# Differential attention with queries on partitions, one set of scores for maxima and exponentials, and both maps combined ahead of the values

## The chip, the core and the metric

The kernel runs on one core of a Trainium2 chip. The metric is the device time of one execution in microseconds (us). The engines are named as in the profile: PE is TensorE (matmuls; PEld its weight loads), DVE is VectorE, ACT is ScalarE, POOL is GpSimd, SP is SyncE, which in this kernel issues every DMA. SBUF is the on-chip memory, PSUM the accumulators: eight banks, each 512 floats wide on 128 partitions.

## The reference

Two layers of a diffusion backbone over 2048 latent tokens and 256 context tokens, width 1024. Layer 0 has a grouped-query attention (stage A) and a neighbourhood attention (B); layer 1 has a differential attention (stage C) and a sliding-window attention (D). Each layer ends with a gated output projection. The change touches stage C, the last part of the program. What is computed there, for 4 heads, 2 maps of 64 columns each, 2304 keys and values of 128 columns:

```python
def diff_attend(q, k, v, lam):
    sc = jnp.einsum('bqhmd,bkhmd->bhmqk', q, k).astype(jnp.float32) * SCALE
    p = jax.nn.softmax(sc, axis=-1)
    a = (p[:, :, 0] - lam * p[:, :, 1]).astype(v.dtype)
    return jnp.einsum('bhqk,bkhe->bqhe', a, v)
# then, for the 2048 latent queries:
yc = (rms_norm(yc, subln) * (1.0 - lam0)).reshape(b, n_tok, -1)
y = jnp.concatenate([yc, yd], axis=-1) * jax.nn.silu(z)
x = x + gate[:, None] * (y @ w_out)
return rms_norm(x, final_norm)
```

## The kernel before

Every number that goes through PE is kept as two float16 halves, a high one (H) and a low one (L, the rest), and a product is made of two or three matmuls of halves that add up in PSUM. All matmuls but transposes go through the helper `mm` (L82).

Stage C is the second half of `layer1`, from `back_pools("C", s)` on. Its work units are (head h, block of 256 queries qb, map m): 4 x 8 x 2 = 64, run by `r_phase` (L800). Each is done in two passes over the scores:

- `r_front` (L736), two units ahead: queries on partitions. Five matmuls of 512 keys with the high half of the keys alone, for each of two tiles of 128 queries (into `pM`), each followed by a maximum on DVE (L752). The maximum is put, negated, into column 64 of a tile Z and brought by a matmul with an identity into row 64 of `Q2`, so that the second pass subtracts it within its matmul.
- `r_scores` (L766): keys on partitions. For each of 18 key tiles two matmuls of 256 queries (`KH` with `Qt`, `KL` with `Q2`), four key tiles to a tile `pS` of two banks, of which there are two. ACT takes the exponential (`Pm`, L778) and casts it to the high half (`H`, L781); POOL subtracts for the low half (`L`, L783). The exponentials lie with keys on partitions, as the product with the values wants them.
- `r_values` (L786), three groups behind: for each key tile and each 128 queries three matmuls of 128 or 129 columns (H with both halves of V, L with the high half) into `pO`. Column 128 of V is one, so that the sum of the exponentials comes with the product.
- `finish` (in `layer1`): divides by the sum. For map 1 it keeps the result times -lambda (`o`, L1454); for map 0 it adds the two (`yc`, L1463), takes the sum of squares, the power -1/2 on POOL (L121), scales and stores.

Between these units a `Filler` lets the output projection run in small steps: `part` (load, gate on POOL, L1494), then `out_pair` (L860: maximum, scaling, transposes, twelve matmuls of 512 columns for each half row, `ot` L911, `xo` L912, and for the last half `final`, L921). Rates (`rateC`, `rateE`, `rateF`) say how many steps come with a group. The order of the instructions on each engine is fixed when the program is built: a scheduler orders them by its own timeline, and on the chip each engine runs its queue in that order and waits at semaphores.

## Time and profile before

| | us |
|---|---|
| median of 3 runs | 3750.49 |
| lowest and highest | 3746.72, 3753.26 |
| the profiled execution's own time | 3762.25 |
| its span, first to last instruction | 3760.40 |
| PE busy | 3565.1 (95%) |
| DVE busy | 2603.6 (69%) |
| ACT busy | 2403.2 (64%) |
| POOL busy | 2347.4 (62%) |

The profile is of one execution. Busy times are sums of instruction durations on an engine. Queries on the trace give them by stretch (windows), by line and shape (groups), or one instruction after another (the timeline). In the groups the part after the bar is busy time and the mean duration of one, then the idle time of the engine just ahead of these instructions and what ended it. A matmul's duration in the records holds its way through the array, so starts that follow each other tell its rate. Stage C fills the last 1000 us of the span.

### The profile page before, as it was taken

How to read it: one execution, taken by the hardware profiler on the slowest of the kernel's cores; microseconds unless marked ns; L12 is line 12 of the kernel's file. 1: busy time of each engine (PE TensorE's matmuls, PEld its weight loads, DVE VectorE, ACT ScalarE, POOL GpSimd, SP SyncE). 2: the span in 40 equal slices, each digit the busy share in tenths (PEclk: the TensorE clock that was granted, in tenths of full speed). 3: DMA queues.
4: the chain of work that ended last, by engine and by line, in shares of the span. 5: the costliest groups of instructions: out<-in, count | busy, mean ns of one | idle time of the engine just before them, and what ended most of it. 6: DMA issues, size and time to landing. Idle time of an engine off the chain costs nothing. (4 is left out here: it accounts for less than half of the span.)

```text
span 3760.4 us, 103033 instructions
## 1 busy us (share of the span) xinstructions
PE 3565.1 (95%) x42242; PEld 2946.7 (78%) x42242; DVE 2603.6 (69%) x6585; ACT 2403.2 (64%) x4094; POOL 2347.4 (62%) x1822
## 2 busy tenths in 40 slices
PE   7869998989999999999999999999989999999998
PEld 5648987878976777677767888999878888887775
DVE  5746779798567676666666888777565656656666
ACT  5215655556668887787864556666567777776665
POOL 3203456676358888788864454435358878877775
PEclk9989999999999999999999999999999999999999
DMA  7884634343261111111135444412351211211222
GB/s 235 214 210 103 124 88 101 80 92 101 67 213 40 44 60 38 48 49 49 33 114 135 104 101 100 105 58 78 113 168 30 78 47 56 62 37 51 101 98 103
DMA packets 455488, 350.64 MB, mean 93 GB/s; under 512 B 207782, under 2 KB 407270, under 8 KB 454502
## 3 DMA queue, kind: packets, MB, share of 16 engines
q1 hardware_dynamic: 455014, 344.06, 33.1%
q8 instruction: 330, 5.41, 0.6%
q14 instruction: 144, 1.18, 0.1%
HBM read 207.43 MB, written 106.90 MB: 84 GB/s over the span
## 5 line engine op out<-in xcount | busy, mean ns | idle before, releaser
L783 POOL TENSOR_TENSOR L<-Pm,H 128x1024 f16<-128x1024 f32 (+1 forms) x640 | 1240.1, 1958 | 293.0 <-ACT H L781 213.1
L82 PE MATMUL pmm<-wk,hT 128*128 128x256 f16 x10848 | 1365.5, 276 | 45.4 <-DVE HL L367 19.3
L82 PEld LDWEIGHTS <-hT 128*128 128x128 f16 x10848 | 1034.9, 99 | 189.6 <-issue 35.9
L752 DVE TENSOR_REDUCE mx<-pM 128x1 f32<-128x512 f32 (+1 forms) x1280 | 787.1, 634 | 514.0 <-PE pM L82 503.8
L82 PE MATMUL pO<-V,H 128*128 128x65 f16 (+3 forms) x9216 | 785.0, 207 | 3.2 <-DVE ya L1260 1.4
L82 PEld LDWEIGHTS <-H 128*128 128x128 f16 x9216 | 644.7, 98 | 100.5 <-DVE o L1454 3.6
L82 PE MATMUL pO<-V,L 128*128 128x65 f16 (+1 forms) x4608 | 710.8, 209 | 8.0 <-POOL L L783 7.4
L514 POOL TENSOR_TENSOR Pl<-Sb,Ph 128x640 f16<-128x640 f32 (+4 forms) x288 | 439.0, 1524 | 427.5 <-ACT Ph L513 248.3
L781 ACT CAST H<-Pm 128x1024 f16<-128x1024 f32 (+1 forms) x640 | 602.9, 959 | 11.8 <-PE pO L82 1.9
L82 PE MATMUL pS<-Qt,KH 128*128 128x256 f16 x2304 | 559.1, 273 | 2.6 <-DMA KH<-qk 1.4
L82 PE MATMUL pS<-Q,KL 65*128 65x256 f16 x2304 | 550.0, 274 | 0.0
L82 PEld LDWEIGHTS <-L 128*128 128x128 f16 x4608 | 442.9, 98 | 53.1 <-POOL L L783 14.9
L82 PE MATMUL pM<-KH,Qt 128*128 128x512 f16 (+1 forms) x1280 | 448.3, 359 | 16.4 <-DVE mx L752 10.3
L778 ACT ACTIVATE Pm<-pS,esc_c 128x1024 f32<-128x1024 f32 (+1 forms) x320 | 323.3, 1026 | 207.9 <-PE pS L82 181.7
L82 PEld LDWEIGHTS <-KL 65*128 65x128 f16 x3824 | 374.4, 98 | 83.3 <-issue 28.2
L778 ACT ACTIVATE Pm<-pS,esc_a 128x1024 f32<-128x1024 f32 (+1 forms) x320 | 324.6, 1027 | 156.1 <-PE pS L82 104.0
L82 PE MATMUL pX<-wo,yT 128*128 128x512 f16 x1488 | 390.2, 380 | 1.5 <-ACT yT L890 1.3
L82 PEld LDWEIGHTS <-KH 128*128 128x128 f16 x2304 | 227.3, 99 | 59.2 <-issue 7.0
L82 PEld LDWEIGHTS <-yT 128*128 128x128 f16 x1632 | 154.2, 98 | 134.4 <-ACT yT L890 6.2
L513 ACT CAST Ph<-Sb 128x640 f16<-128x640 f32 (+4 forms) x288 | 219.4, 762 | 51.1 <-PE pO L82 41.0
L82 PE MATMUL pT<-Q,K 128*128 128x128 f16 x1520 | 216.5, 220 | 18.1 <-ACT Sb L509 6.4
L82 PE MATMUL pT<-Q,KL 65*128 65x128 f16 x1520 | 214.5, 220 | 4.4 <-DVE Q L490 4.4
(295 smaller groups left out, 5536.5 us busy)
## 6 DMA issues: line engine op xcount, KB each, us to landing
qk<-qkst SPq DMA_DIRECT2D x104, 256.0 KB, 2.4
wmod<-w_mod SPq DMA_DIRECT2D x24, 1024.0 KB, 8.4
xo<-x SPq DMA_DIRECT2D x48, 512.0 KB, 3.5
xt<-x SPq DMA_DIRECT2D x34, 512.0 KB, 4.9
G<-zz SPq DMA_DIRECT2D x68, 256.0 KB, 2.5
x<-xo SPq DMA_DIRECT2D x34, 512.0 KB, 2.9
wst<-w_in_even SPq DMA_DIRECT2D x13, 1024.0 KB, 5.8
wst<-w_in_odd SPq DMA_DIRECT2D x13, 1024.0 KB, 5.5
```

The source lines that it names most:

```text
L82: return self.nc.tensor.matmul(out=out, lhsT=l, rhs=r, start=s, stop=e, skip_group_check=skip)
L513: nc.scalar.copy(out=H[:, :n * P], in_=Sb[:, :n * P])
L514: nc.gpsimd.tensor_tensor(out=L[:, :n * P], in0=Sb[:, :n * P], in1=H[:, :n * P], op=ALU.subtract)
L752: nc.vector.tensor_reduce(out=mx[:, j:j + 1], in_=ps[:, :n], op=ALU.max, axis=AX.X)
L778: nc.scalar.activation(out=Pm[:, :n], in_=S[:, :n], func=AF.Exp, scale=esc[0], bias=LNP)
L781: nc.scalar.copy(out=H[:, :n], in_=Pm[:, :n])
L783: eng.tensor_tensor(out=L[:, :n], in0=Pm[:, :n], in1=H[:, :n], op=ALU.subtract)
```

## The change

Stage C gets its own code, with queries on partitions throughout. Its units are (head, tile of 128 queries), 64 of them, each with both maps:

- `c_map`: all 2304 scores of one map for 128 queries, two matmuls per 512 keys (keys' high and low halves, each held twice on 128 partitions, against one query tile that holds both halves), into five banks: `pSa` (1024 columns) and `pSb` (1280). There is one of each. Then three maxima from PSUM, their maximum, the shift, and two exponentials with accumulated sums, into E (32 bit, in SBUF).
- E1 times rho plus E0, with rho = -lambda times the ratio of the sums: columns 0 to 1535 on DVE in two pieces, the rest on POOL in two instructions.
- `c_halves`: of the combined rows, twelve key tiles are cast to H (ACT) and L (POOL) and brought to keys on partitions by four DMA transposes of 128x768; the other six are transposed by PE (`pTr`, one bank), and cast from there by ACT and DVE.
- `c_values`: 18 x 3 matmuls of 128 columns for both maps together, one unit later.
- `finish` scales without a division (the norm takes out the sum); the squares' small term is made on POOL. The filler runs at 5.3 or 5.4 steps a unit. The order of units changes for heads 2 and 3: block by block, so that blocks of all four heads come free early.
- The weights of the output projection come in half rows, the tile `yT` is half as wide, `px` takes turns between `pTr` and `pX` at the end.

Ahead of stage C the program keeps its instructions, but for two small scalars; in layer 1's front some of them change places. The diff, cut to its core:

```diff
-    rateC = 0.55
-    rateE = 2.0
-    rateF = 3.6
+    rateC = (5.3, 5.4)
...
+    DMAK = 12
+
+    def c_pools(self, s):
+        self.pSa = self.pool(s, "pSaC", 1, PSUM)
+        self.pSb = self.pool(s, "pSbC", 1, PSUM)
+        self.pTr = self.pool(s, "pTrC", 1, PSUM)
+        self.pX = self.pool(s, "pXC", 1, PSUM)
+        self.pO = self.pool(s, "pOC", 1, PSUM)
...
+    def c_map(self, u, m, Q, K, esc, shift):
+
+        nc = self.nc
+        S = [self.pSa.tile([P, 1024], F32, name="pSa"), self.pSb.tile([P, 1536], F32, name="pSb")]
+        mx = self.small(f"mx{m}", 3)
+        KH, KL = K
+        for i, (c0, w) in enumerate(((0, 1024), (1024, 1280))):
+            for c in range(0, w, 512):
+                n = min(512, w - c)
+                self.mm(S[i][:, c:c + n], Q, KH[:, c0 + c:c0 + c + n], True, False)
+                self.mm(S[i][:, c:c + n], Q, KL[:, c0 + c:c0 + c + n], False, True)
+        for i, (j, c, w) in enumerate(((0, 0, 1024), (1, 0, 512), (1, 512, 768))):
+            nc.vector.tensor_reduce(out=mx[:, i:i + 1], in_=S[j][:, c:c + w], op=ALU.max, axis=AX.X)
...
+        E = self.wp.tile([P, NTOK], F32, name=f"E{m}", bufs=1 + m)
+        ss = self.small(f"cs{m}", 2)
+        for i, (c0, w) in enumerate(((0, 1024), (1024, 1280))):
+            nc.scalar.activation(out=E[:, c0:c0 + w], in_=S[i][:, :w], func=AF.Exp, scale=esc[0], bias=nb,
+                                 accum_out=ss[:, i:i + 1])
+        return E, ss
+
+    def c_halves(self, E1, E0, rho):
...
+        nc.gpsimd.tensor_scalar(out=E1[:, nd:], in0=E1[:, nd:], scalar1=rho, scalar2=None, op0=ALU.mult)
+        nc.gpsimd.tensor_tensor(out=E1[:, nd:], in0=E1[:, nd:], in1=E0[:, nd:], op=ALU.add)
+        for c0, c1 in ((0, nd // 2), (nd // 2, nd)):
+            nc.vector.scalar_tensor_tensor(out=E1[:, c0:c1], in0=E1[:, c0:c1], scalar=rho, in1=E0[:, c0:c1],
+                                           op0=ALU.mult, op1=ALU.add)
+        for c0, c1 in ((0, nd // 2), (nd // 2, nd)):
+            H = self.wp.tile([P, nd // 2], F16, name="H")
+            L = self.wp.tile([P, nd // 2], F16, name="L")
+            nc.scalar.copy(out=H, in_=E1[:, c0:c1])
+            nc.gpsimd.tensor_tensor(out=L, in0=E1[:, c0:c1], in1=H, op=ALU.subtract)
+            for src, dst in ((H, HT), (L, LT)):
+                nc.sync.dma_start_transpose(out=dst[:, c0 // P:c1 // P], in_=src)
+        for k0 in range(self.DMAK, NT, 4):
+            n = min(4, NT - k0)
+            ps = self.pTr.tile([P, 512], F32, name="pTr")
+            for j in range(n):
+                nc.tensor.transpose(out=ps[:, j * P:(j + 1) * P], in_=E1[:, (k0 + j) * P:(k0 + j + 1) * P], identity=self.idf)
+            pv = ps[:, :n * P].rearrange("p (k x) -> p k x", x=P)
+            nc.scalar.copy(out=HT[:, k0:k0 + n], in_=pv)
+            nc.vector.tensor_tensor(out=LT[:, k0:k0 + n], in0=pv, in1=HT[:, k0:k0 + n], op=ALU.subtract)
+        return HT, LT
+
+    def c_values(self, O, HT, LT, V, kts):
+        for kt in kts:
+            self.mm(O, HT[:, kt], V[:, kt, P:2 * P], kt == 0, False)
+            self.mm(O, HT[:, kt], V[:, kt, 0:P], False, False)
+            self.mm(O, LT[:, kt], V[:, kt, P:2 * P], False, kt == NT - 1)
...
-            self.r_phase([(h, qb, m) for h in range(4) for qb in range(8) for m in (1, 0)], front, back, finish, 128,
-                         ((filler, lambda n: self.rateC if n < 48 else self.rateE if n < 62 else self.rateF),))
...
+            units = [(h, qt) for h in range(2) for qt in range(16)]
+            units += [(h, 2 * qb + t) for qb in range(8) for h in (2, 3) for t in range(2)]
...
+            for n, u in enumerate(units):
...
+                    E1, s1 = self.c_map(u, 1, Qs[1, h, qt // 2][:, q], ks[1], escs[h // 2], shift[1])
+                if pend:
+                    O = self.pO.tile([P, 512], F32, name="pO")[:, 0:P]
+                    self.c_values(O, *pend[1], pend[2], range(0, 9))
+                fill(n, 0.5)
+                r1 = self.small("cr1")
+                nc.vector.tensor_scalar(out=r1, in0=s1[:, 0:1], scalar1=s1[:, 1:2], scalar2=None, op0=ALU.add)
+                nc.vector.reciprocal(out=r1, in_=r1)
+                nc.gpsimd.tensor_scalar(out=r1, in0=r1, scalar1=nlam, scalar2=None, op0=ALU.mult)
+                E0, s0 = self.c_map(u, 0, Qs[0, h, qt // 2][:, q], ks[0], escs[h // 2], shift[0])
+                rho = self.small("rho")
+                nc.vector.tensor_scalar(out=rho, in0=s0[:, 0:1], scalar1=s0[:, 1:2], scalar2=r1, op0=ALU.add, op1=ALU.mult)
+                if pend:
+                    self.c_values(O, *pend[1], pend[2], range(9, NT))
+                    finish(pend[0], O, pend[3])
...
+                halves = self.c_halves(E1, E0, rho)
+                fill(n, 0.5)
+                pend = (u, halves, Vs[h], s0)
```

How the queues stand around this, first on DVE in the middle of stage C before (mx is the maximum of 512 or 256 scores in `pM`, m and Z the maximum of all and its negative, Q the row that goes into `Q2`):

```order
L752 TENSOR_REDUCE mx<-pM 128x1 x5
L755 TENSOR_REDUCE m<-mx 128x1
L758 TENSOR_SCALAR Z_50092<-m 128x1
L752 TENSOR_REDUCE mx<-pM 128x1
L764 CAST Q_59496<-pM 1x256
L752 TENSOR_REDUCE mx<-pM 128x1 x4
```

and on DVE after the change, one unit without filler from the end of its map 1 on (cr and rho are made of the sums; cm and cnb are the maximum of all and the shift; a 1 or 0 in a name is the map; the E1 of the row with x2 and the LT are the unit's before):

```order
L1635 TENSOR_SCALAR cr1_56369<-cs1_56338 128x1
L1636 RECIPROCAL cr1_56369<-cr1_56369 128x1
L1411 TENSOR_REDUCE mx0_56375<-pSa_56373 128x1
L1448 TENSOR_TENSOR LT_56284<-pTr_56301,HT_56283 128x512
L1411 TENSOR_REDUCE mx0_56375<-pSb_56374 128x1 x2
L1448 TENSOR_TENSOR LT_56284<-pTr_56308,HT_56283 128x256
L1413 TENSOR_SCALAR cm0_56389<-mx0_56375 128x1
L1415 TENSOR_SCALAR cnb0_56391<-cm0_56389,nesc_c1_50118,csh0_50094 128x1
L1411 TENSOR_REDUCE mx1_56473<-pSa_56471 128x1
L1640 TENSOR_SCALAR rho_56397<-cs0_56394,cr1_56369 128x1
L1432 SCALAR_TENSOR_TENSOR E1_56337<-E1_56337,rho_56397,E0_56393 128x768 x2
L1411 TENSOR_REDUCE mx1_56473<-pSb_56472 128x1 x2
```

The maxima of a map, which ran two units ahead of the exponentials, now stand between the scores of a map and its own exponentials, and the sums, the combination and the low halves stand between them.

On PE after the change, in the unit that follows, from the last scores of map 0 in `pSa` on (pTr is a transpose of the unit before, pO the values of the unit before):

```order
L80 MATMUL pSa_56527<-KH0_56155,Q0_55626 128x512
L80 LDWEIGHTS Q0_55626
L80 MATMUL pSa_56527<-KL0_56158,Q0_55626 128x512
L1445 MATMUL pTr_56459<-idf_60,E1_56337 128x128 x4
L80 LDWEIGHTS LT_56442
L80 MATMUL pO_56495<-V1_56439,LT_56442 128x128
L80 LDWEIGHTS HT_56441
L80 MATMUL pO_56495<-V1_56439,HT_56441 128x128
```

Sixteen more matmuls of `pO` stand behind these rows before the first one into `pSb` of the same map. The scores of a map, which stood on PE in one piece, now stand on both sides of transposes and of values that come from DMA transposes.

## Rows read from the trace of the kernel before

**Rows 1.** The page, part 1: busy time and share of each engine.
```profile
PE 3565.1 (95%) x42242; PEld 2946.7 (78%) x42242; DVE 2603.6 (69%) x6585; ACT 2403.2 (64%) x4094; POOL 2347.4 (62%) x1822
```
**Rows 2.** Windows: length, busy (count) of PE, PEld, DVE, ACT, POOL; granted clock, DMA.
```profile
3250.00:3500.00 250.00, 247.99 (x2827) 202.65 (x2825) 150.87 (x342) 174.05 (x230) 192.01 (x119) 0.99 0.16 50
```
**Rows 3.** Timeline of PE at the start of stage C; the last value matmul (by tile).
```profile
2755.85 6.81 PE L82 MATMUL pmm<-wk,hT 128*128 128x256 f16 x48 [0.57 <-ACT zz L426]
...
2764.01 0.27 PE L82 MATMUL pS<-Qt,KH 128*128 128x256 f16 x1
...
L82 PE MATMUL pO<-V,L x4608: 191/218/315, 1099.1 to 3735.6; 128*128 128x65 f16 x96, 128*128 128x129 f16 x96
```
**Rows 4.** Groups by shape, 2705 to 3745 us: matmuls of stage C.
```profile
L82 PE MATMUL pO<-V,L 128*128 128x129 f16 x2304 | 432.5, 222 | 3.5 <-POOL L L783 3.4
...
L82 PE MATMUL pS<-Qt,KH 128*128 128x256 f16 x1152 | 278.7, 273 | 2.2 <-DMA KH<-qk 1.4 <-ACT Pm L778 0.7
...
L82 PE MATMUL pM<-KH,Qt 128*128 128x512 f16 x512 | 189.7, 379 | 6.0 <-DVE am L873 4.5 <-DVE mx L752 1.3
```
**Rows 5.** Timeline: PE, and DVE behind it; last row from the chain of waits.
```profile
3300.00 0.38 PE L82 MATMUL pM<-KH,Qt 128*128 128x512 f16 x1
...
3300.41 0.69 DVE L752 TENSOR_REDUCE mx<-pM 128x1 f32<-128x512 f32 x1 [0.79 <-PE pM L82]
...
3304.75 0.81 PE L82 MATMUL pX<-wo,yT 128*128 128x512 f16 x3
...
3717.31 0.66 PE L886 MATMUL pM<-idf,ya 128*128 128x128 f32 x4 [0.61 <-ACT ya L883]
...
3669.44 1.26 PE pO L82 x22
```
**Rows 6.** Groups by shape, 2705 to 3745 us: DVE, ACT and POOL, work that remains in another shape.
```profile
L783 POOL TENSOR_TENSOR L<-Pm,H 128x1024 f16<-128x1024 f32 x256 | 550.7, 2167 | 156.2 <-ACT H L781 125.4 <-issue 9.9 <-PE pO L82 7.7
...
L752 DVE TENSOR_REDUCE mx<-pM 128x1 f32<-128x512 f32 x512 | 344.1, 687 | 264.6 <-PE pM L82 261.6
L778 ACT ACTIVATE Pm<-pS,esc_c 128x1024 f32<-128x1024 f32 x256 | 282.2, 1112 | 205.4 <-PE pS L82 179.5 <-POOL L L783 17.1 <-PE pO L82 4.3
...
L781 ACT CAST H<-Pm 128x1024 f16<-128x1024 f32 x256 | 264.1, 1043 | 5.1 <-PE pO L82 1.5
...
L783 POOL TENSOR_TENSOR L<-Pm,H 128x512 f16<-128x512 f32 x64 | 75.1, 1173 | 0.1
...
L752 DVE TENSOR_REDUCE mx<-pM 128x1 f32<-128x256 f32 x128 | 53.6, 419 | 29.2 <-PE pM L82 28.3
L778 ACT ACTIVATE Pm<-pS,esc_c 128x512 f32<-128x512 f32 x64 | 43.7, 683 | 2.5 <-PE pS L82 2.2
...
L755 DVE TENSOR_REDUCE m<-mx 128x1 f32<-128x5 f32 x128 | 20.1, 157 | 3.9
...
L1465 ACT ACTIVATION_READ_ACCUMULATOR cj<-yc 128x1 f32 x64 | 12.3, 192 | 0.0
```
**Rows 7.** Groups by shape, 2705 to 3745 us: DVE work of the filler.
```profile
L911 DVE SCALAR_TENSOR_TENSOR ot<-pX,am,gate 128x512 f32<-128x512 f32 x57 | 42.7, 749 | 16.0 <-PE pX L82 15.6
...
L891 DVE SCALAR_TENSOR_TENSOR yT<-pX,yT 128x512 f16<-128x512 f32 x27 | 18.5, 684 | 7.6 <-ACT yT L890 7.5
```
**Rows 8.** DVE with two operands in SBUF: duration ns min/median/max, first and last start, forms.
```profile
L929 DVE SCALAR_TENSOR_TENSOR xo<-xo,frs,fn x16: 1266/1285/3094, 3536.6 to 3755.6; 128x1024 f32<-128x1024 f32 x16
...
L1319 DVE SCALAR_TENSOR_TENSOR wo<-wst,wsc_wo,wo x16: 1269/1874/3242, 1107.7 to 2812.2; 128x1024 f16<-128x1024 f32 x16
```
**Rows 9.** DMA transposes of 128x512 and less: on SP, to landing, one pair and its follower.
```profile
L333 SPq DMA_TRANSPOSE qkst<-HL x244: 1167/1248/8486, 64.4 to 2399.9; - x122
...
qkst<-HL SPq DMA_TRANSPOSE x244, 2.5
...
80.50 2.50 SPq L333 DMA_TRANSPOSE qkst<-HL  x2
...
84.29 0.38 SPq L335 DMA_DIRECT2D qk<-qkst  x1
```

More of the change, by code (lines that the diff above doesn't have):

```diff
@@ L855, in px @@
         self.pxi += 1
+        if self.late and self.pM is None:
+            return (self.pTr if self.pxi % 2 else self.pX).tile([P, 512], F32, name=("pX", "pTr")[self.pxi % 2])
         if self.late and self.pxi % 3:
@@ L858, in px, with out_pair @@
         return self.pX.tile([P, 512], F32, name="pX")
-    def out_pair(self, l, p, y2, W, gate, ks=range(8), src=None, xos=None, dst=None, base=0, maxima=None):
+    def out_pair(self, l, p, y2, W, gate, ks=range(8), src=None, xos=None, dst=None, base=0, maxima=None, ts=(0, 1)):
         nc = self.nc
@@ L867, in out_pair @@
         out = []
-        for t in range(2):
+        for t in ts:
             yg = y2[t]
@@ L1197, in layer0 @@
         with ExitStack() as s:
[L1198 removed]
+            wo, kv = self.back_pools(s)
             K = {}
@@ new lines, in c_keys, with c_vals @@
+    def c_keys(self, h, pool):
+        nc, r = self.nc, []
+        for m in (1, 0):
+            K = []
+            for part, n in ((slice(0, 64), "H"), (slice(64, 128), "L")):
+                t = pool.tile([P, NTOK], F16, name=f"K{n}{m}")
+                for b in range(2):
+                    nc.sync.dma_start(out=t[64 * b:64 * b + 64], in_=self.qk[1][8 + 2 * h + m, part])
+                K.append(t)
+            r.append(K)
+        return {1: r[0], 0: r[1]}
+    def c_vals(self, h):
+        V = self.wp.tile([P, NT, 257], F16, name=f"V{h % 2}", bufs=1)
+        self.nc.sync.dma_start(out=V, in_=self.vC[h])
+        return V
@@ L1486, in part, with rows2 @@
+            self.late, self.pxi = False, 0
+            self.x2 = [self.dp.tile([256, DM], F32, name=f"x2_{p}") for p in range(8)]
+            last = []
+            def rows2(x, qb):
+                return lambda t: x[qb][t * P:(t + 1) * P, :]
             def part(qb, k0, k1, src, dst):
-                c = slice(k0 // 4 * 512, k0 // 4 * 512 + 512)
+                c = slice(k0 * P, k1 * P)
                 n = (k1 - k0) * P
@@ L1496, in part @@
[L1496 to L1502 removed]
+                yield from self.out_pair(1, qb, ys, self.W, lambda: gate[0], range(k0, k1), src, None, dst, k0)
@@ new lines, in before_last @@
+            def before_last():
+                yield from part(7, 0, 3, rows2(self.x2, 7), None)
+                xos = self.xos
+                for t in range(2):
+                    gl = self.gp.tile([P, 512], F32, name=f"gl{t}")
+                    nc.sync.dma_start(out=gl[:, :P], in_=self.rows(self.G[1], 7, t)[:, 384:512])
+                    last.append((xos[t], gl, self.yp.tile([P, 512], F32, name=f"ya{t}")))
+            for qb in range(8):
+                filler.add(part(qb, 4, 8, lambda t, qb=qb: self.src_rows(1, qb, t), rows2(self.x2, qb)))
@@ new lines, in layer1, with queries @@
+            units = [(h, qt) for h in range(2) for qt in range(16)]
+            units += [(h, 2 * qb + t) for qb in range(8) for h in (2, 3) for t in range(2)]
+            pend = None
+            credit = 0.0
+            def queries(n):
+                if n >= len(units):
+                    return
+                h, qt = units[n]
+                if qt % 2 == 0:
+                    for m in (1, 0):
+                        q = self.qp.tile([P, 256], F16, name=f"Q{m}")
+                        nc.sync.dma_start(out=q, in_=self.qk[1][2 * h + m, :, qt * P:(qt + 2) * P])
+                        Qs[m, h, qt // 2] = q
@@ L1503, in layer1 @@
+            O = self.pO.tile([P, 512], F32, name="pO")[:, 0:P]
+            self.c_values(O, *pend[1], pend[2], range(NT))
+            self.late = True
+            finish(pend[0], O, pend[3])
             filler.drain()
```

218 lines of the change are left out of this document (119 added, 99 removed).

## Prediction

> **What bounds the kernel now.** The page first [rows 1]: PE is busy 95% of the span, the others 62 to 69%. An average says nothing of one stage, so the windows come next: in 250 us in the middle of stage C PE is busy 247.99 us at a granted clock of 0.99, POOL 192, ACT 174, DVE 151 [rows 2]. PE is the bound there, and the idle columns of the groups agree: the value and score matmuls lost 2 to 4 us in the whole stage, while DVE's maxima waited 262 us for PE [rows 4, 6]. The timeline gives the stage's ends: its first scores start at 2764.0 us, behind the last 48 projection matmuls of layer 1's front, and its last value matmul at 3735.6 us [rows 3]. That is 972 us for 64 pairs of (head, 128 queries), 15.2 us for a pair, which after the change is the unit. Behind the last value 25 us are left to the end of the span (3760.4).
>
> **What the change takes from PE.** A link of 22 value matmuls takes 1.26 us, 0.057 us for one; three of 512 columns take 0.81 us, so that with 0.38 us for one alone they follow each other at 0.215 us; four transposes take 0.66 us [rows 4, 5]. Removed: the maxima's scores (512 x 0.215 us, and 128 of half that width, 124 us) and, of 6912 value matmuls, half (3456 x 0.057 = 197 us). The scores proper stay at 247 us: 2304 of 256 columns become 1024 of 512 and 256 of 256. Added: 384 transposes, at 0.165 us at most, 63 us. PE's work falls by some 260 us. If PE stayed the bound, a unit would take about 11 us. It will not: the scores of a map now have one buffer, and its exponentials need the maximum of all of them, so the unit becomes a chain over four engines. I work out that chain.
>
> **One map.** Scores of `pSa` (four matmuls): 3 x 0.215 + 0.38 = 1.02 us. Maxima: 256 and 512 columns took 0.42 and 0.69 us, so 1.05 us per 1000 columns and 0.15 us fixed; 1024 columns are 1.24, 512 are 0.69, 768 are 0.96, together 2.89 us; those of `pSb` hide no matmul, since its scores are ready before the first maximum ends. Combining and shift: 2 x 0.157 = 0.31 us. Exponential of 1024: 1.11 us [rows 5, 6]. Only then may PE write `pSa` again. A handover is short: DVE's maximum at 3300.41 us starts 0.03 us behind the matmul that began at 3300.00. With three of them a map takes 5.42 us, a unit's two **10.8 us**.
>
> **What stands in that chain besides.** It is read from DVE's order, since DVE runs in order and a row between two links is a link.
> - After map 1's shift stand the sum and the reciprocal. They wait for both exponentials and their accumulator reads: 1.11 + 0.19 + 1.35 + 0.19 us, the exponential of 1280 from those of 512 and 1024 [rows 6]. The scores of map 0 would be ready after 1.11 + 1.02 us. With the two operations themselves (0.31 us) the loss is 1.0 us in 56 of 64 units: **0.9 us**.
> - rho and two combinations of 768 columns (E1 rho + E0) stand between the maxima of `pSa` and `pSb`, or just ahead of them. rho is 0.16 us. The nearest rows for the others are DVE operations on two operands in SBUF: of 1024 columns, 1.28 us at the median in L929 and 1.87 us in L1319, with maxima of 3.09 and 3.24 us [rows 8]. L929 waits for POOL's power and so runs mostly with POOL idle, L1319 runs beside POOL's subtractions. For 768 columns that is 1.0 or 1.4 us, at worst 2.4. POOL's first product starts on the same rho, so I take 1.4 us for the first; beside the second POOL waits for a cast part of the time, 1.2 us: **2.75 us** in all, with ends of 2.2 and 5.0.
> - The low halves from PSUM (512 and 256 columns, 0.68 and 0.42 us after L891 and the narrow maximum) stand in the chain in 48 and 45 of 64 units: **0.8 us** [rows 6, 7].
> - The filler's DVE work is some 125 us. By the order 73 us of it stand between a map's first maximum and its shift (19 `ot`, 22 maxima and 27 `yT` halves of about 0.7 us each, half weights, and final steps), the rest where DVE waits for an exponential: **1.1 us** a unit [rows 7].
>
> Sum: 10.8 + 0.9 + 2.75 + 0.8 + 1.1 = **16.4 us** a unit, against 15.2 now.
>
> The Trainium skill (GPSIMD Engine Reference, the table of the specifications) says that GpSimd shares its SBUF interfaces with VectorE, with contention where a DVE instruction has two SBUF inputs. The trace agrees with 1.28 against 1.87 us [rows 8]. By that rule both combinations would slow, 0.2 us more in the unit.
>
> **What is covered.** ACT: four exponentials and their reads 5.7 us, two casts of 768 columns 1.6 us (1.04 us for 1024), two from PSUM, a copy, a square and a scaling some 2.3 us, filler 1.1 us: 10.7 of 16.4. POOL: two subtractions of 768 (1.67 us each by the 512 and 1024 rows), a sum of about the same, a product whose price no row shows (0.3 to 1.9 us, I take 1.1), small operations 1.9 us, filler 2 us: 10 us [rows 6]. DVE is busiest with 13 us. PE has 10 to 11 us. None is full; they hide behind the chain. SP gets four transposes a unit: 1.25 us each for up to 512 columns, 2.5 us to landing [rows 9]; with the stores and loads some 8 us of SP. Their cover is a unit's length, but a thin one: values of the unit before stand on PE between `pSa` and `pSb` of map 0. From rho to the landing of the first low half I count 1.4 (combination), 0.8 (cast), 1.7 (subtraction), the rest of two transposes ahead (0.9), 2.6: 7.4 us. From rho to the end of the scores of `pSa`, behind which those values stand, the chain takes 2.6 + 1.65 + 0.3 + 1.1 + 1.0 = 6.7 us. With 18 values (1.0 us) the scores of `pSb` begin at 8.4 us, though `pSb` is free at 7.2 us; the first 512 are there at 9.0 us. DVE, kept by the sum, ends its maximum of `pSa` then too (4.55 to the shift, 2.85 to the sums, 0.3, 1.25). So this wait costs nothing as long as transposes land within 2.6 us, and each microsecond beyond is one in the chain; I add nothing, and the range has it.
>
> **The ends.** The 25 early maxima scores (5 us) leave the front, which ends PE-bound, so stage C starts at 2758 us. After the last map's shift there follow exponentials (2.9), rho, combination, casts, DMA transposes and the last values, some 13 us, and then what stood behind the last value before, 25 us; less 3 us, as one tile of 128 queries ends alone. So the end is 2758 + 64 T + 35 us. T = 15.1 us would change nothing. T = 16.4 gives a span of 3843 us, against 3760.4, **83 us more**; the profiled execution's own time is 3762.25, 11.8 above the median of the runs (3750.49), so 3845 - 12 = **3833 us** is the forecast. With T from 15.2 to 17.5, its own range is 3756 to 3903 us.
>
> **Rivals.**
> 1. *Faster: the chain holds less than its rows.* If DVE's combinations run at 1.0 us, and filler and low halves fall into gaps (where DVE waits for values to let PE go on, they cost nothing), T is 10.8 + 0.9 + 2.2 + 0.2 = 14.1 us: 2758 + 902 + 35 = 3695, **3685 us**. It decides when less than 15.1 us of work stands in the chain, 1.3 us below my sum. For it: 50 us of the filler already stand in gaps, and L929 shows 1.28 us. Against it: 10.8 + 0.9 is fixed by buffers and order, and the order has the low halves in the chain. Chance 0.29.
> 2. *No change*, T within 0.12 us of 15.1: 0.06.
> 3. *Slower still: transposed halves come late.* Were each block of 128x128 to cost what the pair in the trace allows, 3.79 us for 8 blocks, 0.47 us [rows 9], 24 of them take 11.4 us a unit; the queue would hold, but the first low half would land 3 us later, and PE's scores with it: T about 18.4, **3961 us**. Against it: 512 columns land 2.5 us after issue, which leaves 1.25 us of transfer. Chance 0.14, with T from 17.5 on.
> 4. *The transposes as the bound.* Only at more than 0.65 us a block would they need a whole unit; the pair excludes it. Chance 0.01. The Trainium skill (VectorE: DVE Perf Modes, The three transpose paths) gives 1.309 us for one 128x128 block by DMA, against 0.39 us on TensorE. One after the other, 24 blocks would take 31 us a unit, and the kernel some 1000 us longer; the trace contradicts it as a rate.
>
> **How the numbers follow.** A measurement of this kernel can tell about 0.2% (7.5 us) from no change. The forecast case (T 15.2 to 17.5) has a chance of 0.50, rivals 3 and 4 0.15 together: slower 0.65; same 0.06; faster 0.29. The range of 8 in 10 reaches into the faster rival to 3685 us, which leaves out about 1 in 8, and to T = 18, 3935 us, which leaves out 1 in 12.
>
> **What would show it.** PE no longer full in the middle of stage C: about 10.5 of 16.4 us, 65%. DVE's waits named after exponentials and PE's scores, and ACT's exponentials waiting for the shift (`cnb`). In the middle 16 to 17 us between first scores of successive units; some 15 where no filler runs (the units after the first 32). E1 rho + E0 at 1.0 to 1.5 us. DMA transposes of 768 columns at 1.3 us on SP, landing within 3 us. I would be wrong if units came every 14 us or less (then the buffers are not the chain), if transposes land after more than 4 us, or if PE's granted clock fell well below the 0.99 of now.

## The result, and the profile after

The changed kernel takes 4005.11 us (median of 4 runs, 4003.0 to 4010.3), the kernel before 3751.27 in the same comparison: a ratio of 1.0671, 95% interval 1.0658 to 1.0684. The forecast was 3833 us, its range ended at 3935: the direction was right, the size was not. The profiled execution has a span of 4008.2 us.

The page, parts 1 and 2, and the waits of PE (engine, line, what it waited for: us, times, longest):

```profile
PE 3442.4 (86%) x37378; PEld 2679.9 (67%) x37378; DVE 2757.8 (69%) x6515; ACT 2334.3 (58%) x4294; POOL 2304.9 (58%) x2015
...
PE   7879989899989999999899999996677677677666
...
PEclk9989999999999999999999999998788888778888
...
PE pO L80 <- DMA HT<-H: 195.0, 57, 7.5
PE pSa L80 <- ACT E L1419: 69.6, 58, 5.7
PE pX L80 <- DVE yT L891: 29.6, 22, 4.5
PE pTr L1445 <- POOL E L1430: 22.3, 11, 5.2
PE pO L80 <- DMA LT<-L: 20.5, 20, 2.9
```

PE's row and its clock fall together in the last 13 slices, which are stage C. A window of 250 us in it (columns as in [rows 2]):

```profile
3000.00:3250.00 250.00, 174.19 (x1243) 106.70 (x1244) 153.07 (x265) 124.68 (x225) 148.83 (x139) 0.83 0.44 105
```

PE is busy 174 us instead of 248 [rows 2], at a granted clock of 0.83 instead of 0.99, and the other engines have 153 us (DVE) or less. So no engine is full: the stage became a chain, as forecast, but a longer one. Groups by shape, 2705 to 3970 us, that answer to [rows 6], and the DMA transposes, which answer to [rows 9]:

```profile
L1438 POOL TENSOR_TENSOR L<-E,H 128x768 f16<-128x768 f32 x126 | 207.2, 1653 | 1.9 <-ACT H L1437 1.9
L1429 POOL TENSOR_SCALAR E<-E,rho 128x768 f32<-128x768 f32 x63 | 168.6, 2676 | 7.2 <-DVE rho L1640 3.3 <-PE pSb L80 1.8 <-DVE am L873 0.4
L1432 DVE SCALAR_TENSOR_TENSOR E<-E,rho,E 128x768 f32<-128x768 f32 x128 | 160.6, 1292 | 1.3
L1411 DVE TENSOR_REDUCE mx<-pSa 128x1 f32<-128x1024 f32 x128 | 156.1, 1220 | 95.2 <-PE pSa L80 91.5
L1419 ACT ACTIVATE E<-pSa,cnb,esc_c 128x1024 f32<-128x1024 f32 x128 | 154.0, 1203 | 160.5 <-DVE cnb L1415 155.1 <-DVE ar L877 5.2
...
L1411 DVE TENSOR_REDUCE mx<-pSb 128x1 f32<-128x768 f32 x128 | 120.8, 944 | 0.0
...
L1411 DVE TENSOR_REDUCE mx<-pSb 128x1 f32<-128x512 f32 x128 | 87.3, 682 | 48.2 <-PE pSb L80 47.8
...
L1413 DVE TENSOR_SCALAR cm<-mx 128x1 f32<-128x1 f32 x128 | 34.2, 267 | 1.9
```

```profile
L1419 ACT ACTIVATE E<-pSa,cnb,esc_c x128: 1185/1204/1212, 2765.1 to 3965.4; 128x1024 f32<-128x1024 f32 x128
...
L1440 SPq DMA_TRANSPOSE HT<-H x128: 1209/1212/1980, 2778.6 to 3972.0; - x128
...
DMA to landing us min/median/max: 2.7/2.8/5.2
```

The first row of the last fence gives the unit: 128 exponentials of `pSa`, two a unit, from 2765.1 to 3965.4, are 1200.3 / 127 = 9.45 us a map and **18.9 us a unit**, where the prediction had 16.4. 64 x 2.5 = 160 of the 172 us that are missing are this; the two ends were right in sum (2758 + 64 x 18.9 + 35 = 4003, the span is 4008). What is to be explained is 2.5 us of a unit.

### The profile page after: what moved, and what is told of

Its sections match the earlier page's. It is cut to its first block, busy times and chain, and to the rows that moved or that the text cites. A ratio compares the mean times of both kernels' runs of the same rounds, so it can differ in the third digit from the quotient of the medians.

```text
span 4008.2 us, 94016 instructions
## 1 busy us (share of the span) xinstructions
PE 3442.4 (86%) x37378; PEld 2679.9 (67%) x37378; DVE 2757.8 (69%) x6515; ACT 2334.3 (58%) x4294; POOL 2304.9 (58%) x2015
## 3 DMA queue, kind: packets, MB, share of 16 engines
q14 instruction: 149, 1.22, 0.1%
## 5 line engine op out<-in xcount | busy, mean ns | idle before, releaser
L781 POOL TENSOR_TENSOR L<-Pm,H 128x1024 f16<-128x1024 f32 (+1 forms) x320 | 617.9, 1954 | 133.4 <-ACT H L779 82.9
L750 DVE TENSOR_REDUCE mx<-pM 128x1 f32<-128x512 f32 (+1 forms) x640 | 393.6, 634 | 218.8 <-PE pM L80 212.6
L80 PE MATMUL pO<-V,HT 128*128 128x128 f16 x2304 | 266.6, 239 | 196.4 <-DMA HT<-H 195.0
L80 PE MATMUL pO<-V,H 128*128 128x65 f16 (+1 forms) x4608 | 305.6, 193 | 1.4 <-DVE ya L1260 1.1
L779 ACT CAST H<-Pm 128x1024 f16<-128x1024 f32 (+1 forms) x320 | 302.2, 960 | 6.2 <-PE pO L80 0.3
L80 PEld LDWEIGHTS <-H 128*128 128x128 f16 x4608 | 264.9, 98 | 52.2 <-DVE ya L1260 2.8
L80 PE MATMUL pO<-V,L 128*128 128x65 f16 x2304 | 277.4, 196 | 4.0 <-POOL L L781 3.6
L80 PE MATMUL pS<-Qt,KH 128*128 128x256 f16 x1152 | 279.5, 273 | 0.3 <-ACT Pm L776 0.3
L80 PE MATMUL pS<-Q,KL 65*128 65x256 f16 x1152 | 275.6, 274 | 0.0
L80 PE MATMUL pO<-V,LT 128*128 128x128 f16 x1152 | 238.4, 239 | 31.0 <-DMA LT<-L 20.5
```

Of the source, the lines that this page charges most:

```text
L80: return self.nc.tensor.matmul(out=out, lhsT=l, rhs=r, start=s, stop=e, skip_group_check=skip)
L750: nc.vector.tensor_reduce(out=mx[:, j:j + 1], in_=ps[:, :n], op=ALU.max, axis=AX.X)
L779: nc.scalar.copy(out=H[:, :n], in_=Pm[:, :n])
L781: eng.tensor_tensor(out=L[:, :n], in0=Pm[:, :n], in1=H[:, :n], op=ALU.subtract)
```

## The experiments

Units are worked out for all runs as just shown, and their two parts from the starts of all 128 exponentials: map 1's part runs from the start of map 0's exponential in the unit before to the start of its own, map 0's part from there (both means; the recorded expectations have some of them up to 0.04 us off). Clock is the granted clock of 3000 to 3250 us. Ratios are to the kernel before, which ran beside each. The runs without filler (e8 to e11, e13) are one execution each: their whole time is longer, since the filler then runs behind the units, and only their units are compared.

| run | us | ratio, 95% | unit | map 1 | map 0 | clock |
|---|---|---|---|---|---|---|
| changed kernel | 4005 | 1.0658-1.0684 | 18.90 | 9.47 | 9.43 | 0.83 |
| e1 values later | 4015 | 1.0677-1.0709 | 18.95 | 9.10 | 9.84 | 0.84 |
| e2 busy PE | 4019 | 1.0677-1.0718 | 19.11 | 9.33 | 9.78 | 0.92 |
| e3 product behind | 4004 | 1.0646-1.0677 | 18.76 | 9.49 | 9.28 | 0.85 |
| e4 combine in exp | 3945 | 1.0487-1.0518 | 17.70 | 9.67 | 8.04 | 0.86 |
| e5 values behind | 3972 | 1.0565-1.0600 | 18.46 | 9.84 | 8.62 | 0.86 |
| e6 behind and busy | 3942 | 1.0481-1.0513 | 17.95 | 9.59 | 8.37 | 0.96 |
| e7 combine and behind | 3882 | 1.0316-1.0347 | 16.73 | 7.95 | 8.77 | 0.91 |
| e8 no filler beside | 4329 | - | 18.11 | 8.58 | 9.52 | 0.77 |
| e9 e8, busy | 4246 | - | 16.86 | 8.58 | 8.28 | 1.00 |
| e10 e8, values behind | 4255 | - | 16.91 | 8.52 | 8.38 | 0.80 |
| e11 e8, both | 4208 | - | 16.26 | 8.65 | 7.62 | 0.99 |
| e12 all by DMA | 3887 | 1.0328-1.0362 | 17.04 | 7.77 | 9.26 | 0.88 |
| e13 e8, both, 16 | 4219 | - | 16.39 | 9.26 | 7.15 | 0.97 |
| e14 third buffer | 3855 | 1.0247-1.0277 | 16.46 | 7.77 | 8.69 | 0.86 |
| e15 e14, busy | 3834 | 1.0189-1.0223 | 16.22 | 7.18 | 9.03 | 0.97 |
| e16 values split | 3903 | 1.0385-1.0416 | 17.30 | 8.50 | 8.80 | 0.88 |
| e17 scalings off ACT | 3918 | 1.0425-1.0460 | 17.45 | 8.69 | 8.77 | 0.87 |

### Four first tries (e1 to e4)

e1, values a unit later and rho with its combinations half a unit later:
```diff
+                if half:
+                    done = (half[0], combine(*half[1:]), Vs[half[0][0]], half[4])
                 fill(n, 0.5)
...
-                halves = self.c_halves(E1, E0, rho)
...
-                pend = (u, halves, Vs[h], s0)
+                pend = done if half else None
+                half = (u, E1, E0, r1, s0)
```


> rho and the two combinations are written half a unit later (behind map 1's scores of the next unit), and the values of a unit are taken two units later, so that PE never stands before transposed halves that have not landed. Theory A (the halves come late: PE waited 226 us in stage C for HT and LT, and these waits stand ahead of map 0's scores): those waits go, map 0's first score starts 0.15 us behind its release instead of 0.6, and its second block about 1 us earlier; a unit falls from 18.9 to 16.9-17.4 us, 3880-3920 us. Theory B (the clock: map 0's scores run at the lower of TensorE's levels, 0.427 us instead of 0.215 a matmul, because PE stood idle before them): PE is as idle before map 0's scores as it was, so a unit stays at 18.5 us or more, 3980-4010 us.

Measured 18.95 us. It did not test the theory: in the order that the scheduler made, two values still stood ahead of map 0's scores, and PE's waits for HT stayed (225.5 us). To delay an instruction in this kernel its inputs must be late, not its place in the text.

e2, in the loop, ahead of the first values:
```diff
+                    for i in range(16):
+                        self.mm(O4[:, P:P + 384], Qs[0, h, qt // 2][:, q], ks[0][0][:, 0:384])
                     self.c_values(O, *pend[1], pend[2], range(0, 9))
```


> The changed kernel with 16 more matmuls of 384 columns a unit, on keys and queries that are there, written to columns of the pO bank that nothing reads, behind map 1's scores; they fill PE's idle time before map 0's scores (2.6 us of 4.5 at the full clock) and add nothing else. Theory B (the clock): map 0's scores go to 0.215 us a matmul, 2.1 us less for the ten of them, of which 1.5 us stand in the chain; a unit falls to 17.4 us, about 3910 us. Theory A (late halves): the halves land as late as before; no gain, 4000 us, or up to 1 us a unit more where the added matmuls outlast the wait, 4070 us.

The clock rose to 0.92 and the time did not fall. By its expectation that speaks against the clock alone. But map 0's first block ran at the full rate in only 30 of 64 units (in the changed kernel in 6), and late halves, filler and added matmuls stand in one queue, so it settles little.

e3, the two POOL lines of `c_halves` written behind the loop over its halves:


> The changed kernel with POOL's product and sum (E1 rho + E0 of the last 768 columns) written behind its two subtractions. Theory A with the product as the cause (2.7 us on POOL between rho and the first subtraction, which the prediction left out): the first low half lands 1.5-2 us earlier, 7 us behind rho instead of 9; a unit falls by 0.5-1 us, 3940-3975 us. Where the product is not the cause (theory B, or the halves late for another reason): within 10 us of 4005, or slower, since the six tiles transposed on PE then come 3 us later.

4004 us, no change, but the order on POOL was hardly touched (the product is ready first), so it is no evidence on the product.

e4, e1's edit (half a unit later) and rho made to wait for the shift of the next unit's map 1; against e1:
```diff
+                nc.vector.tensor_scalar(out=z, in0=self.nb, scalar1=0.0, scalar2=s0[:, 0:1], op0=ALU.mult, op1=ALU.add)
-                nc.vector.tensor_scalar(out=rho, in0=s0[:, 0:1], scalar1=s0[:, 1:2], scalar2=r1, op0=ALU.add, op1=ALU.mult)
+                nc.vector.tensor_scalar(out=rho, in0=z, scalar1=s0[:, 1:2], scalar2=r1, op0=ALU.add, op1=ALU.mult)
```


> As the first of these, and rho made to wait for the next unit's map 1 shift (one more small operation on DVE that adds nothing to it), so that the two combinations run while DVE waits for map 1's exponentials, and not between a map's maxima. If a unit is the chain of two maps that the prediction took, with the combinations, rho and most of the low halves out of it: 2 x 5.8 us (the measured links without waits), 1 us where the combinations outlast the exponential, 1 us of low halves and filler: 13.7 us, 3690 us (3640 to 3780, the upper end if map 0's scores stay at the lower clock): faster than the kernel before. If the chain is not the bound, but the late halves or something that both share: over 3850 us.

3945 us, far above its range: 1.2 us a unit less, and not where expected. Map 0's part fell to 8.04 us (in nearly all units of this order nothing stands between the blocks of its scores), and map 1's stayed at 9.67 without the combinations, since PE began its scores some 2 us behind their release, kept by values that waited for halves. That pointed to PE's queue.

### The unit without filler (e8 to e11, e13)

To see a unit clean, e8 lets the filler run behind the last unit (`filler.step()` left out of `fill`).


> The changed kernel with the whole filler (output weights, gates and output products of layer 1) run behind the last unit instead of beside the units. The time gets longer and is not the point; the spacing of the units is. By the prediction (1.1 us of a unit's chain): 17.8 us instead of 18.9. If the filler costs what its DVE work in the chain and its matmuls ahead of the scores amount to, over 2 us, a unit takes 16.5 us or less; if the chain waits for halves that land late, the filler is hidden behind them, and a unit stays above 18.3 us.

18.11 us, with the same order in nearly all units (map 0's part takes from 8.8 to 10.9 us in it, but for the first unit). One unit of e8, with a part of 8.99 us, PE:

```profile
3308.59 0.58 PE L80 MATMUL pSa<-KH,Q 128*128 128x512 f16 x1 [0.98 <-ACT E L1419]
...
3309.82 0.63 PE L80 MATMUL pSa<-KL,Q 128*128 128x512 f16 x1
3310.25 1.06 PE L1445 MATMUL pTr<-idf,E 128*128 128x128 f32 x4
3311.10 0.31 PE L80 MATMUL pO<-V,LT 128*128 128x128 f16 x1
...
3312.40 0.38 PE L80 MATMUL pSb<-KH,Q 128*128 128x512 f16 x1
...
3313.37 0.27 PE L80 MATMUL pSb<-KL,Q 128*128 128x256 f16 x1
...
3317.58 0.38 PE L80 MATMUL pSa<-KH,Q 128*128 128x512 f16 x1 [1.55 <-ACT E L1419]
...
3318.22 0.38 PE L80 MATMUL pSa<-KL,Q 128*128 128x512 f16 x1
```

And DVE, from the reciprocal between the maps on; behind it a row of the waits of e8 and the same row of the changed kernel (us, times, longest):

```profile
3310.22 0.17 DVE L1635 RECIPROCAL cr<-cr 128x1 f32<-128x1 f32 x1
3310.49 1.22 DVE L1411 TENSOR_REDUCE mx<-pSa 128x1 f32<-128x1024 f32 x1
3311.96 0.69 DVE L1448 TENSOR_TENSOR LT<-pTr,HT 128x512 f16<-128x512 f32 x1 [0.25 <-ACT HT L1447]
3313.68 1.55 DVE L1411 TENSOR_REDUCE mx<-pSb 128x1 f32<-128x512 f32 x2 [1.03 <-PE pSb L80]
...
DVE mx L1411 <- PE pSb L80: 95.3, 63, 2.4
...
DVE mx L1411 <- PE pSb L80: 47.8, 40, 3.4
```

Map 0's four matmuls of `pSa` start 0.41 us apart (3308.59 to 3309.82), map 1's 0.21 us (3317.58 to 3318.22): TensorE's 1.2 and 2.4 GHz. Ahead of map 0's PE had stood nearly idle from the end of map 1's scores, some 5 us; ahead of map 1's it had worked, but for 1.55 us. Then, between the blocks of map 0, four transposes and 18 values take from 3310.25 to 3312.40, 2.15 us in which `pSb` is free. DVE ends the maximum of `pSa` at 3311.71, has one low half, and waits 1.03 us for the scores in `pSb`; over all units of e8 it waits 95.3 us for them, 1.5 us a unit. In the changed kernel these waits are 47.8 us, 0.75 a unit: there values stand between the blocks of map 0 in 30 of 64 units, not in 62. And the maximum of the first 512 columns of `pSb` starts behind the last matmul of the whole tile (3313.37), not behind its own two.

e9 keeps PE busy, e10 holds the values behind map 0's first maximum, e11 does both:
```diff
+                    self.behind_max(O4)
+                    for i in range(30):
+                        self.mm(O4[:, P:P + 384], Qs[0, h, qt // 2][:, q], ks[0][0][:, 0:384])
```
```diff
+    def behind_max(self, O4):
+        self.nc.tensor.transpose(out=O4[0:1, P:2 * P], in_=self.mx[:, 0:1], identity=self.idf)
...
-                    self.c_values(O, *pend[1], pend[2], range(0, 9))
...
-                    self.c_values(O, *pend[1], pend[2], range(9, NT))
+                    self.behind_max(O4)
+                    self.c_values(O, *pend[1], pend[2], range(NT))
```


> As the run without filler (units of 18.1 us, of which map 0's part is 9.56 and map 1's 8.57), with 30 matmuls of 384 columns a unit that nothing reads, behind map 1's first maximum and ahead of the values, to keep PE busy until map 0's scores; the 18 values stay between the two blocks of map 0's scores. If the clock is what makes these blocks late: scores, values and second block at twice the rate, maxima of the second block 1.8 us earlier, a unit 16.3 us (16.0 to 16.6). If late halves make them late: no change, 18.0 us or more.

> As the run without filler, with the values behind both blocks of map 0's scores (the four transposes on PE stay between the blocks in every second unit). The clock is left as it is. If what stands between the blocks is the loss: the second block starts 0.8 to 2.9 us earlier; a unit 16.9 us (16.6 to 17.3). If only the clock is the loss: above 17.8 us.

> Both at once, with 24 matmuls of 512 columns. If the two together are what the prediction missed, a unit without filler is the chain that it worked out: 16.4 less 1.1 for the filler, 15.3 us (15.0 to 15.7). If more was missed than these two: over 16 us.

Windows of e9 and of e10, for the clock (0.77 in e8), in this order:

```profile
3000.00:3250.00 250.00, 203.98 (x1656) 129.30 (x1655) 155.74 (x252) 132.67 (x240) 137.30 (x135) 1.00 0.33 70
```
```profile
3000.00:3250.00 250.00, 160.73 (x1206) 103.34 (x1206) 149.89 (x247) 131.10 (x234) 131.92 (x132) 0.80 0.33 69
```

16.86 us (above its range) and 16.91 us (within it): each alone gives back 1.2 us, all of it in map 0's part (9.52 to 8.28 and 8.38). e10 leaves the clock nearly where it was (0.80), so what stands between the blocks costs by itself. In 31 of its units the four transposes and the low half still stand there and only the values are gone: map 0's part takes 8.74 us in these in the mean, 9.58 in the 62 units of e8 with all three, so the values alone cost 0.84 us. In the other 32 it takes 8.10. e9 does not show what the clock costs by itself: in its order the four transposes fell behind the second block, and on DVE, in 63 of 64 units, the sum and the reciprocal behind the maximum of `pSa` and the low half behind those of `pSb`.

e11 missed its range: 16.26 us, units of 14.8 and 17.2 us in turn. e13 is e11 with 16 instead of 24 added matmuls.


> As the run without filler that had both (values behind map 0's scores, 24 added matmuls), with 16 added matmuls. If the 24 themselves held up every second unit by 2.4 us: all units near the shorter ones, 14.8 to 15.5 us, which is the chain that the prediction worked out without filler (15.3). If something else makes every second unit longer: 14.8 and 17.2 us in turn as before.

Also missed, 16.39 us, but its parts tell why. Map 0's part is 7.15 us, near what the prediction had for it (5.42 + 0.9 + 0.8 = 7.12), though not by the same links: sum and reciprocal stand behind the maximum of `pSa` here too, in 63 of 64 units. Map 1's part rose from 8.58 to 9.26: the values, no longer between the blocks of map 0's scores, now stand ahead of map 1's, and there their low halves are late (PE waits 48.5 us for them, 0.8 a unit). PE in e13:

```profile
3312.49 0.23 PE L80 MATMUL pO<-V,LT 128*128 128x128 f16 x1 [1.79 <-DMA LT<-L]
...
3314.44 0.38 PE L80 MATMUL pSa<-KH,Q 128*128 128x512 f16 x1
```

So the 24 matmuls alone were not what made e11's long units; a wait for low halves stood ahead of map 1's scores.

### The same with the filler (e5, e6, e7)

e5 is e10's edit on the changed kernel, e6 adds 12 matmuls behind map 1's first maximum, e7 puts e5's hold on e4, behind map 1's maximum of the unit after next.


> The changed kernel with all values of the unit before held, by one transpose on PE that reads map 0's first maximum, behind map 0's scores; nothing else is moved. (The first of the experiments did not test theory A: the waits for HT stayed, 226 us, since the order still has two value matmuls ahead of map 0's scores.) Theory A (late halves, and behind them the values that stand between the blocks of map 0's scores): the waits for HT and LT go; map 0's second block of scores starts 0.3 us behind its release instead of 1.9; map 0's part of a unit falls from 9.45 to 8.1 us, a unit to 17.5, 3915 us (3880 to 3940). Theory B (the clock alone): the halves were hidden, and map 0's scores stay at 0.427 us a matmul: 3990 to 4015 us.

> As the one before, and 12 matmuls of 512 columns a unit that nothing reads, behind map 1's first maximum, in PE's idle time before map 0's scores (2.6 us at the full clock). Theory B on top of A: map 0's scores at 0.215 us a matmul, 0.9 us less in the chain for the first block: 55 us below the run before. If the clock costs nothing that is not hidden: within 15 us of the run before; if the added matmuls outlast the gap: slower than it.

> The combinations in map 1's exponential as in the fourth experiment, whose units still lost 2.06 us before map 1's scores (values waiting for halves ahead of them), and the values held behind map 1's first maximum of the unit after next. If late halves in PE's order were the loss: map 1's scores start 0.15 us behind their release, map 1's part of a unit falls from 9.65 to 7.5 us, a unit to 15.5, about 3800 us (3720 to 3840, the upper end if map 1's scores then run at the lower clock). If not: 3930 to 3960 us.

e5 gained 0.44 us, a third of what theory A had expected, and its 3972 us lie between the two forecasts. Its waits of PE, and of DVE for `pSb`:

```profile
PE pSa L80 <- ACT E L1420: 194.5, 58, 7.0
PE pX L80 <- DVE yT L891: 63.8, 26, 4.7
PE pTr L1446 <- POOL E L1431: 45.0, 13, 6.5
...
DVE mx L1411 <- PE pSb L80: 18.7, 28, 0.9
```

The 195 us for HT are gone, and PE waits as long for the exponential instead (194.5, before 69.6). So the waits for HT were mostly time in which map 0's scores could not have started anyway: the largest row of PE's waits was hidden, and theory A, as far as it is these waits, falls as the main cause. What e5 gained is what DVE no longer waits for `pSb` (47.8 to 18.7 us, 0.45 a unit). Map 1's part rose from 9.47 to 9.84: values stand ahead of its scores instead. e6 lies 30 us below e5 (expected 55) with the clock at 0.96; both edits together give back 0.95 us a unit. e7 came to 3882 us, above its range: PE now stood 126.9 us before transposes for POOL's sum.

### Towards a version that beats the kernel before (e12, e14 to e17)

e12 is e7 with all 18 tiles combined on DVE in three pieces and transposed by DMA:
```diff
+        parts = [(c, c + 768) for c in (0, 768, 1536)]
+        for c0, c1 in parts:
             nc.vector.scalar_tensor_tensor(out=E1[:, c0:c1], in0=E1[:, c0:c1], scalar=rho, in1=E0[:, c0:c1],
...
-        nc.gpsimd.tensor_scalar(out=E1[:, nd:], in0=E1[:, nd:], scalar1=rho, scalar2=None, op0=ALU.mult)
-        nc.gpsimd.tensor_tensor(out=E1[:, nd:], in0=E1[:, nd:], in1=E0[:, nd:], op=ALU.add)
```


> The combinations in map 1's exponential and the values behind map 1's maximum, as in the seventh experiment (16.74 us a unit, where PE still waited 127 us for the sum on POOL ahead of the transposes on PE), and all 18 tiles combined on DVE in three pieces of 768 columns and transposed by DMA: no product and no sum on POOL, no transposes on PE, no low halves from PSUM; the bank that they leave serves the filler. Two maps' chain 11.6, combinations beyond the exponential 1.5, map 1's scores at the lower clock 0.8, filler 1.0: 14.9 us, 3765 us (3700 to 3840). If the transposes of 24 instead of 16 blocks by DMA hold up the values: over 3850 us.

3887 us, no gain over e7 and above its range. ACT in e12:

```profile
3321.45 0.83 ACT L1437 CAST H<-E 128x768 f16<-128x768 f32 x1 [3.52 <-DMA HT<-H]
3322.18 1.20 ACT L1420 ACTIVATE E<-pSa,cnb,esc_c 128x1024 f32<-128x1024 f32 x1
```

The third cast waits for one of two buffers, whose transpose is under way, and map 0's exponential stands behind it. e14 gives it a third buffer (`name="H", bufs=3`); e15 adds eight matmuls behind map 0's first maximum.


> As the run with all tiles by DMA, with three buffers instead of two for the cast high halves (and one instead of two for the weights that the filler loads at the start of the stage). If the third cast, which waits 1.8 to 3.5 us for its buffer and stands ahead of map 0's exponentials on ACT, held the unit: 1.5 to 2 us less, 15.0 to 15.5 us a unit, 3775 us (3740 to 3810). If the lower clock or POOL holds it: above 16.5 us, 3850 us or more.

> As the one before, and 8 matmuls of 512 columns a unit that nothing reads, behind map 0's first maximum, in PE's idle time before map 1's scores. If the lower clock costs what it did without filler (map 1's first block 0.85 us, the values 1.3 us, which delay map 0's scores by about 0.8 us): 1.3 to 1.6 us less a unit than the run before, 13.7 to 14.2 us, 3690 us: faster than the kernel before. If PE's added work collides with the filler's: no gain over the run before.

e14 gained 0.6 us of the 1.5 to 2 expected; e15 another 0.24 of 1.3 to 1.6. At 3834 us it is the fastest version here and still 2% slower than before. Exponentials of ACT in e15, where no filler runs beside:

```profile
3303.43 1.21 ACT L1420 ACTIVATE E<-pSa,cnb,esc_c 128x1024 f32<-128x1024 f32 x1 [1.62 <-DVE cnb L1416]
...
3309.68 1.20 ACT L1420 ACTIVATE E<-pSa,cnb,esc_c 128x1024 f32<-128x1024 f32 x1 [3.27 <-DVE cnb L1416]
...
3316.64 1.21 ACT L1420 ACTIVATE E<-pSa,cnb,esc_c 128x1024 f32<-128x1024 f32 x1 [1.62 <-DVE cnb L1416]
```

Map 0 at 3303.43, map 1, map 0 again at 3316.64: 13.2 us a unit, below the 15.1 at which nothing changes. Six units of e15 have no filler beside them, and five of these take 13.2 or 13.3 us. The mean of all is 16.2.

e16 splits the values over both of PE's gaps (the second half held by a matmul that adds zero), e17 also moves two scalings from ACT to POOL:
```diff
+                    nc.vector.tensor_scalar(out=z16, in0=self.mx[:, 0:1], scalar1=0.0, scalar2=None, op0=ALU.mult)
+                    self.mm(O[:, 0:1], pend[1][0][:, 0], z16, False, False)
                     self.c_values(O, *pend[1], pend[2], range(9, NT))
```


> As the run with the third buffer, no added matmuls that nothing reads; instead the values are split: one half behind map 1's first maximum as before, the other behind map 0's (one matmul that adds zero, made from that maximum, holds them), so that values stand in both of PE's gaps. If values that end late hold map 0's scores and an idle PE lowers the clock of map 1's: map 0's scores start 0.2 us behind their release instead of 0.93, map 1's run at 0.215 us a matmul, a unit 15.4 us, 3785 us (3750 to 3810). If the filler's own work holds the units: 16 us or more, 3820 us or more.

> As the one before, and the scaling of a unit's result and of the filler's inputs on POOL instead of ACT, so that ACT no longer waits for POOL's and DVE's small results ahead of its exponentials. If these waits are in the chain: 0.3 to 0.5 us less a unit than the run before, 15.0 us, about 3755 us, the time of the kernel before. If they are hidden, or POOL's added work (some 2 us a unit) is late for others: no gain or some loss.

Both got slower, e16 than e14 and e17 than e16. In e16 the small operation that makes the zero fell behind the maxima of `pSb` in DVE's order, so the held half came late and delayed map 1's scores (its part 8.50 instead of 7.77 us). In e17 either ACT's waits on small results were hidden or POOL's added work cost what they gave; no run tells which. What the filler's 3 us a unit in e15 consist of stays open: no run here takes it apart.

## Why the prediction was right in direction and wrong in size

- **PE no longer the bound**: right. 70% busy was forecast as 65%.
- **One map, 5.42 us**: a little short. Without any wait its links in e8 are 1.06 (scores at the full clock), 1.22 + 0.68 + 0.94 (maxima, forecast to 0.05), 0.5 (combining and shift; forecast 0.31 from a row of another form), 1.20 (exponential; forecast 1.11), and some 0.2 for handovers: 5.8 us.
- **Sum and reciprocal, 0.9 us**: about right. In e8 they end at 3310.39, 0.74 us behind the time at which scores at the full clock would have let the maximum of `pSa` start (3308.59 + 1.06). The maximum starts at 3310.49, as its slow scores end, so these two delays lie over each other.
- **rho and two combinations, 2.75 us**: right in the mean, 0.27 + 2 x 1.29 = 2.85.
- **Filler, 1.1 us**: 18.90 less 18.11 is 0.8, all of it in map 1's part (9.47 and 8.58).
- **"This wait costs nothing as long as transposes land within 2.6 us"**: this step failed. It put at nothing what stands on PE between the blocks of map 0's scores. The transposes were nearly as forecast (1.21 us on the queue, landing after 2.8 us). But the sentence counted 18 values at the full clock (1.0 us), left out the four transposes that stand there too, and let the maximum start on the first 512 columns. In e8 DVE waited 1.5 us a unit for `pSb`, in the changed kernel 0.75. In the unit of e8 shown above the maximum of `pSb` starts 5.2 us behind the end of map 1's exponential (3307.24 + 1.20 to 3313.68); by the prediction's count it would have been 3.4 us (9.0 and 5.65 us behind rho), or 4.1 with the low half that it had in another term.
- **The way of the first low half, 7.4 us from rho to landing**: short, by the product on POOL, which was taken at 1.1 us and beside the path. In the same unit it takes 2.97 us and ends 1.2 us behind the cast for which the subtraction waits:

```profile
3302.23 0.27 DVE L1639 TENSOR_SCALAR rho<-cs,cr 128x1 f32<-128x1 f32 x1
...
3302.67 2.97 POOL L1429 TENSOR_SCALAR E<-E,rho 128x768 f32<-128x768 f32 x1
3305.61 1.63 POOL L1438 TENSOR_TENSOR L<-E,H 128x768 f16<-128x768 f32 x1
...
3307.31 1.24 SPq L1440 DMA_TRANSPOSE LT<-L  x1
```

  With 2.8 us to landing that is 7.9 us. It was not the loss in this unit, since the half lands at 3310.1 and PE reaches the first value that reads it at 3311.10. In the changed kernel the way takes 9.2 us in the mean; e3, which was to test the product, did not.
- **PE's clock**: named only as what would make the prediction wrong, with no price. At the lower level map 0's first block lets its maximum start 0.84 us later than map 1's (1.90 and 1.06 us from its first start), but the sum and the reciprocal would have held that maximum for 0.74 us of it anyway. What the clock costs besides, it costs in the wait for `pSb`. An estimate from the rows of that unit: at the full clock the second block would start some 1.5 us earlier (0.8 from the first block, 0.4 from the transposes, 0.3 from the values), more than the 1.03 us that DVE waits there. No run shows the clock's cost by itself.

The sum of it: without filler the prediction's unit was 15.3 us, 8.17 for map 1 and 7.12 for map 0. e8 has 8.58 and 9.52. So 2.4 us are map 0's part, 0.4 the small links of map 1's, less 0.3 for the filler: 2.5. Of the 2.4, 1.5 are DVE's wait for `pSb`; the rest lies in small links and in the low half ahead of `pSb`'s maxima, which waits 0.25 us for its cast. That the order on PE makes much of this wait is shown by e10 (0.84 us for the values alone), and that order and clock together can take map 0's part to 7.15 by e13, with the sum and the reciprocal moved too. The clock's share is not shown, and the two 1.2 us of e9 and e10 do not add up: both take from one and the same wait.

With the filler this account holds only in part: both edits together give back 0.95 us there (e6), and 1.5 us a unit above the forecast stay open. The trace of the changed kernel points at one place: the first scores of a map start 0.61 us (map 0) and 0.78 us (map 1) behind the exponential that frees `pSa`, in the mean, against 0.21 and 0.14 in e8. Of 56 starts that are over 0.3 us late, 42 come behind values of the unit before and 11 behind the filler's matmuls; the prediction counted the filler's work in the chain on DVE alone. How much of this stands in the chain, no run shows.

The rivals: 1 (14.1 us) needed a chain with less in it than the rows, and it had more. 3 came nearest in time (18.4 us), by another mechanism: it had transposes at 0.47 us a block, and six blocks took 1.21 us; and e5 shows that taking PE's waits for the halves away leaves PE waiting for the exponential.

The Trainium skill (GPSIMD Engine Reference, the table of the specifications) has DVE instructions with two SBUF inputs contend with POOL. The trace agrees: in e12, 159 of 192 combinations ran mostly with POOL idle and took 1.02 us in the mean, 13 ran beside its subtractions and took up to 2.40; in the changed kernel the median is 1.02 us, the mean 1.29.

## What to carry to other kernels

When a change takes an engine off its bound, price what is left on it at the clock that it gets when it idles, if it is TensorE, and look at what its queue holds between the links of the new chain: work that was free beside a full engine is then in the chain. The largest wait of an engine is not its loss: take it away, and see what it waits for next. And an experiment that moves an instruction must make its input late or early; where a scheduler orders the program, the place in the text moves little.

## What the runs showed of the hardware that was not expected

- TensorE ran at one of two rates, 0.427 or 0.215 us for matmuls of 512 columns one behind the other. The Trainium skill (TensorE: Matmul & The Clock Gate, Wait — 56ns, not 53.3ns?) gives 426.7 and 215.7 ns for the cold and the warm array; the trace agrees. With 30 matmuls a unit that compute nothing the kernel without filler was 1.2 us a unit faster, though other instructions changed places with them.
- A product with a scalar per partition on POOL (768 columns) took 2.68 us on average, 2.21 at the least, longer than its sum of two tensors (1.80 at the median).
- A DMA transpose of 128x768 took 1.21 us on SP's queue and landed after 2.7 us at the least: no dearer than those of 512 columns in the kernel before [rows 9].
